# A fused encoder layer on one core: the FFN's matmul operands in two float16 parts with scales found on the chip, in place of two float32r parts

## The chip, the cores and the metric

One core of one Trainium2 chip runs the whole layer in one launch. The metric is device time in microseconds of that core, the median over timed runs. Engines are named as in the profile: PE (matmuls), PEld (weight loads of PE), DVE, ACT, POOL, and SP, which here only issues DMAs. "The DVE queue" and the like mean that an engine takes its instructions in one fixed order, so that an instruction that waits holds up all that stand behind it.

## What is computed

Sequence 1024, model width 1024, float32 in and out. The layer is an attention part (two kinds of heads, not touched here), a projection back to 1024, and then the part that this case is about:

```python
hn = rmsnorm(h, norm_ffn)
g = hn @ w_gate                      # 1024 x 2816
u = hn @ w_up                        # 1024 x 2816
g = conv3_depthwise(g, conv_w) + conv_b
h = h + (silu(g) * u) @ w_down       # 2816 x 1024
out = rmsnorm(h, norm_final)
```

The result has float32 accuracy, which one low-precision matmul doesn't give. So each operand is split into a high and a low part, and each block product is three matmuls: high times high, high weight times low operand, low weight times high operand.

## The kernel before

**Tiles.** Activations lie transposed: 128 features on the partitions, 1024 tokens along the row, in two halves of 512. Gate and up are taken together as a 2x2 block product by a scheme with seven products in place of eight (Strassen's, in a form with few sums). The same is done for the down projection. The 22 tiles of 128 hidden features ("units", class `Gated`) each take seven groups of matmuls, `p1` to `p7`, with 4 blocks of 128 in a group and three matmuls in a block (`group`, lines 956 to 961). That is 22 x 7 x 4 x 3 = 1848 matmuls with 512 columns. The down projection is seven products over 4 output tiles and 11 hidden tiles: 7 x 4 x 11 x 3 = 924 matmuls, the last 66 of them cut in two halves of 256 columns.

**Splits.** `split_w` (line 943) makes the two parts of a weight: ACT copies the float32 tile into a float32r tile (the high part, line 948), and DVE subtracts that from the float32 tile (the low part, line 949). `operand` (line 963) does this for the normalised activations, and `x_split` (line 1274) for the gated activations, which go through DRAM (`keep`, `x_load`) between the two projections. The sums that the seven products need (`ws`, `sum`, `t23`, `t4`) are DVE subtractions and additions ahead of the splits.

**Stages of the part in question**, with their place in the profile: the second half of the output projection with the residual and its sum of squares (lines 1017 to 1042; about 367 to 419 us); four head units taken phase by phase, while the activations of the second half of the tokens are still being made (to about 498 us); 18 units one after the other, each of which also prepares the weights of the next (class `Weights`, one step between two groups; to about 842 us); the down projection, where weights and gated activations are loaded some steps ahead (to 1051 us); and the final norm.

**What sets the order.** PE runs in program order (`manual_schedule` for PE). A scheduler orders the other engines' instructions and the DMAs of each queue when the program is built. Weights come through 9 buffers for the high and 9 for the low parts. PSUM banks have tags with two buffers each: `pj`, `o`, `s`, `pt`. In the down projection, product 1 adds onto the bank that still holds product 0, and product 0 itself is copied out for later use (`leave`).

Of the kernel before, what the change touches and what calls it, by code (L numbers as in the profile page):

```python
# [22 lines left out]
KT = D // 128  # L23
# [33 lines left out]
V_TOP, P_TOP, TINY = 2.0 ** 14, 2.0 ** 15, 1e-30  # L57

# [3 lines left out]
def hybrid_layer(tc, xT, w_in, w_out, w_gate, w_up, w_down, small, sink, rpb, consts, rope, out):  # L62
    nc = tc.nc
    with ExitStack() as ctx:
# [17 lines left out]
        def tmp(name, dt=F32, n=S):  # L82
            return tpool.tile([128, n], dt, name=name, tag="t", padded_shape=[128, S + 2])

# [858 lines left out]
        def split_w(src, n):  # L943

            pad = [128, 4, 128]
            hi = fpool.tile([128, n, 128], F32R, name="whi", tag="wh", bufs=9, padded_shape=pad)
            lo = fpool.tile([128, n, 128], F32R, name="wlo", tag="wl", bufs=9, padded_shape=pad)
            nc.scalar.activation(hi, src, AF.Copy)  # L948
            nc.vector.tensor_tensor(lo, src, f32(hi[:, :, :]), op=ALU.subtract)  # L949
            return [(hi[:, j, :], lo[:, j, :]) for j in range(n)]  # L950

        def load_raw(src, n):
            raw = fpool.tile([128, n, 128], F32, name="raw", tag="raw", bufs=3, padded_shape=[128, KT, 128])
            nc.sync.dma_start(raw, src)
            return raw

# [6 lines left out]
        def operand(src, tag):  # L963

            t = big("hg", tag, F32R)
            nc.scalar.activation(t[:, 0:HALF], src, AF.Copy)
            nc.vector.tensor_tensor(t[:, HALF:S], src, f32(t[:, 0:HALF]), op=ALU.subtract)
            return t[:, 0:HALF], t[:, HALF:S]
# [17 lines left out]
        def normed(h, wide, ds):  # L986
            for d in ds:
                nc.vector.scalar_tensor_tensor(at(d, h), at(d, h), col(C_NFFN + d), wide, op0=ALU.mult, op1=ALU.mult)

        def pure(f):  # L990
            raw = load_raw(w_gate[f], KT)
            W[f, "11"], W[f, "12"] = split_w(raw[:, 0:4], 4), split_w(raw[:, 4:8], 4)
# [8 lines left out]
        def head_weights(i, name):  # L1001
# [15 lines left out]
            W[f, name] = split_w(t, 4)  # L1017

        for h in range(2):
            for d in range(KT):  # L1020
# [9 lines left out]
                if h == 0 and d in (3, 4):  # L1030
                    pure((0, FT // 2)[d - 3])
                if h == 0 and d >= 5 or h == 1 and d == 0:
                    head_weights((d - 5) % KT, "s1")
# [10 lines left out]
        class Weights:  # L1044


            def __init__(self, f):
                self.f = f
                self.steps = [self.load, self.w11, self.w12, self.s1, self.s2, self.s4, self.s3, self.a22]

            def put(self, name, src):
                W[self.f, name] = split_w(src, 4)

            def load(self):
                self.g, self.u = load_raw(w_gate[self.f], KT), load_raw(w_up[self.f], KT)
# [33 lines left out]
        class Gated:  # L1089
# [32 lines left out]
            def conv(self):  # L1122
                f, gs = self.f, self.gs
                cw = lambda i: col(C_CW + 3 * f + i)
# [439 lines left out]
```

## Time and profile before

| | us |
|---|---|
| median of 3 runs (lowest, highest) | 1068.71 (1068.39, 1070.65) |
| the profiled execution, whole | 1067.82 |
| its span, first to last instruction | 1065.9 |
| PE busy | 1042.1 |
| DVE busy | 853.8 |
| ACT busy | 553.9 |
| POOL busy | 212.2 |

The mean granted clock of PE is 0.996. "Busy" is the time in which at least one instruction of the engine ran, by the profile's records. PE's records overlap, since matmuls are pipelined: a 512-column matmul is recorded with 0.39 us, while the next one starts 0.23 us after it. So matmuls are costed by the distance of their starts, and DVE's and ACT's instructions, which overlap a little too, by the length of an unbroken run of them divided by its count.

### The profile page before, as it was taken

To read this page: it belongs to the slowest core of one execution; us is meant where nothing else is said; L and a number is where in the kernel's file an instruction comes from. 1 tells how busy PE (TensorE), PEld (TensorE's weight loads), DVE (VectorE), ACT (ScalarE), POOL (GpSimd) and SP (SyncE) were. 2 spreads that over 40 slices of the span, in tenths; PEclk is the share of its full clock that TensorE was granted. 3 is DMA by queue.
4 is the path that set the end of the run, shared out by engine and by line. 5 is a ranking of instruction groups with operands and counts; after the bars stand their busy time and mean duration, and the time that the engine had idled before them with its cause. 6 is when DMAs were issued, how large, how long until landed. Compare 5 with 4: busy or idle time off the path is not lost.

```text
span 1065.9 us, 15180 instructions
## 1 busy us (share of the span) xinstructions
PE 1042.1 (98%) x4998; PEld 844.6 (79%) x4998; DVE 853.8 (80%) x1670; ACT 553.9 (52%) x1047; POOL 212.2 (20%) x312
## 2 busy tenths in 40 slices
PE   9989999999999999999999999999999999999997
PEld 7876777777777777787888888888888888888887
DVE  7789998767896789899988887887787858996764
ACT  8167787767686354454443433434334645544441
POOL 2234545767886200000000000000000000000002
PEclk9999999999999999999999999999999999999999
DMA  7236564877788273123433322223232789866644
GB/s 276 71 91 145 109 133 97 163 148 139 138 178 207 87 246 140 48 79 148 174 122 110 127 91 109 99 89 113 95 128 98 257 274 292 288 218 228 216 145 158
DMA packets 137358, 161.86 MB, mean 152 GB/s; under 512 B 76608, under 2 KB 87872, under 8 KB 137280
## 3 DMA queue, kind: packets, MB, share of 16 engines
q1 hardware_dynamic: 126624, 135.15, 45.0%
q10 hardware_dynamic: 10656, 25.76, 6.4%
q8 instruction: 39, 0.64, 0.2%
q14 instruction: 39, 0.32, 0.1%
HBM read 103.45 MB, written 28.57 MB: 124 GB/s over the span
## 4 chain that ended last, share of the span: by engine, by line
PE 69%; DVE 9%; DMA 2%; ACT 1%; issue 1%; POOL 1%; SPq 0%; DVEq 0%; ACTq 0%; POOLq 0%
PE dn L959 7%; PE dn L960 7%; PE dn L961 7%; PE z L961 5%; PE z L959 5%; PE z L960 5%; PE pj L157 4%; PE pj L159 4%; PE pj L158 4%; PE x L959 3%; PE x L960 3%; PE x L961 3%; PE y L961 3%; PE y L959 3%; PE y L960 3%; PE s L388 2%
## 5 line engine op out<-in xcount | busy, mean ns | idle before, releaser
L1385 POOL TENSOR_TENSOR h<-h,wide 128x256 f32<-128x256 f32 (+1 forms) x6 | 5.4, 919 | 624.7 <-ACT wide L1381 624.7
L948 ACT ACTIVATE whi<-ws 128x512 fp32r<-128x512 f32 (+1 forms) x100 | 60.2, 623 | 128.9 <-DVE ws L1065 82.5
L959 PE MATMUL dn<-xd,whi 128*128 128x512 f32 (+1 forms) x330 | 124.1, 376 | 0.0
L960 PE MATMUL dn<-xd,whi 128*128 128x512 f32 (+1 forms) x330 | 123.8, 375 | 0.0
L961 PE MATMUL dn<-xd,wlo 128*128 128x512 f32 (+1 forms) x330 | 123.7, 375 | 0.0
L157 PE MATMUL pj<-xgh,whi 128*128 128x512 f32 x248 | 107.2, 432 | 0.7 <-ACT whi L149 0.7
L961 PE MATMUL z<-hg,wlo 128*128 128x512 f32 x264 | 103.1, 390 | 0.6 <-DVE wlo L949 0.6
L959 PE MATMUL z<-hg,whi 128*128 128x512 f32 x264 | 103.0, 390 | 0.0
L960 PE MATMUL z<-hg,whi 128*128 128x512 f32 x264 | 102.8, 389 | 0.0
L159 PE MATMUL pj<-xgh,wlo 128*128 128x512 f32 x248 | 98.3, 396 | 1.4 <-POOL wlo L150 1.4
L158 PE MATMUL pj<-xgl,whi 128*128 128x512 f32 x248 | 97.9, 395 | 0.0
L422 ACT ACTIVATE p<-p,nm 128x385 f32<-128x385 f32 (+3 forms) x128 | 74.8, 585 | 39.7 <-DVE nm L418 34.8
L949 DVE TENSOR_TENSOR wlo<-ws,whi 128x512 fp32r<-128x512 f32 (+1 forms) x100 | 66.6, 680 | 18.1 <-ACT whi L948 18.0
L949 DVE TENSOR_TENSOR wlo<-raw,whi 128x512 fp32r<-128x512 f32 (+1 forms) x90 | 58.7, 673 | 22.7 <-ACT whi L948 20.8
L948 ACT ACTIVATE whi<-raw 128x512 fp32r<-128x512 f32 (+1 forms) x90 | 53.8, 615 | 38.6 <-DMA raw<-in_w_down_dram 10.4
L1277 ACT ACTIVATE xd<-xd 128x512 fp32r<-128x512 f32 x77 | 47.0, 625 | 46.4 <-DMA xd<-x 45.8
L960 PEld LDWEIGHTS dn<-xd,whi 128*128 128x128 f32 x330 | 62.1, 188 | 11.3 <-DVE xd L1278 0.2
L959 PEld LDWEIGHTS dn<-xd,whi 128*128 128x128 f32 x330 | 62.1, 188 | 11.2
L961 PEld LDWEIGHTS dn<-xd,wlo 128*128 128x128 f32 x330 | 62.1, 188 | 11.1
L1278 DVE TENSOR_TENSOR xd<-xd 128x512 fp32r<-128x512 f32 x77 | 51.8, 686 | 22.8 <-ACT xd L1277 22.6
L961 PE MATMUL y<-hg,wlo 128*128 128x512 f32 x176 | 68.7, 391 | 0.5 <-DVE wlo L949 0.5
L959 PE MATMUL x<-hg,whi 128*128 128x512 f32 x176 | 68.7, 390 | 0.0
(231 smaller groups left out, 2690.7 us busy)
## 6 DMA issues: line engine op xcount, KB each, us to landing
xd<-x SPq DMA_DIRECT2D x77, 256.0 KB, 4.7
raw<-in_w_down_dram SPq DMA_DIRECT2D x64, 256.0 KB, 3.9
raw<-in_w_gate_dram SPq DMA_DIRECT2D x22, 512.0 KB, 3.3
raw<-in_w_up_dram SPq DMA_DIRECT2D x22, 512.0 KB, 3.6
x<-c ACTq DMA_DIRECT2D x22, 512.0 KB, 2.7
raw<-in_w_in_dram SPq DMA_DIRECT2D x32, 256.0 KB, 3.2
raw<-in_w_down_dram SPq DMA_DIRECT2D x32, 192.0 KB, 4.0
x<-t ACTq DMA_DIRECT2D x11, 512.0 KB, 2.7
```

The costliest lines, as they stand in the source:

```text
L157: nc.tensor.matmul(ps, w[0], x[0][:, tsl(h)], start=first, stop=False)
L158: nc.tensor.matmul(ps, w[0], x[1][:, tsl(h)], start=False, stop=False)
L159: nc.tensor.matmul(ps, w[1], x[0][:, tsl(h)], start=False, stop=last)
L388: nc.tensor.matmul(ps[:, 0:n], qs, k[i][:, cs[0] * 128:cs[0] * 128 + n], start=i == 0, stop=i == 1)
L422: nc.scalar.activation(p[:, 0:e], p[:, 0:e], AF.Exp, bias=nm, scale=-1.0, accum_out=sm)
L948: nc.scalar.activation(hi, src, AF.Copy)
L949: nc.vector.tensor_tensor(lo, src, f32(hi[:, :, :]), op=ALU.subtract)
L959: nc.tensor.matmul(ps, w[0], x[0], start=first and i == 0, stop=False, skip_group_check=True)
L960: nc.tensor.matmul(ps, w[0], x[1], start=False, stop=False, skip_group_check=True)
L961: nc.tensor.matmul(ps, w[1], x[0], start=False, stop=last and i == len(ws) - 1, skip_group_check=True)
L1277: nc.scalar.activation(hi, f32(lo), AF.Copy)
L1278: nc.vector.tensor_tensor(lo, f32(lo), f32(hi), op=ALU.subtract)
```

## The change

Every operand of the FFN's and the down projection's matmuls becomes float16, still in two parts, and the three matmuls of a block stay. Since float16 has a small range, the operands are brought to fixed sizes by powers of two that are found on the chip:

- **Gate and up weights.** `weigh(f)` loads both 128x1024 weight tiles of a hidden tile a second time (`scan_rows`: a DMA on SP, and an ACT `Square` with a row sum); POOL adds the two sums. `settle_scale(f)` takes the largest over all partitions (`spread_max`: a transpose on PE, a reduction on DVE), forms the power -1/2 on POOL, and cuts the result to a power of two on DVE (`exponent`). It then forms `back` (its inverse) and `taps` (the convolution's weights times `back`) on DVE and POOL. `split_w` multiplies by the scale while it splits: ACT with a scale from a tile, DVE with `SCALAR_TENSOR_TENSOR` in place of `TENSOR_TENSOR`.
- **Norm gains.** `scale_gains` brings the FFN norm's gains to a fixed size, once; `operand` then splits the normalised activations without a scale, into a float16 pair.
- **Down weights.** One scale for all of `w_down`: 24 scans, two in each unit, and one `joint`.
- **Gated activations.** Each unit's result gets one more ACT `Square` with a row sum. Two scales come from these sums: one from all tiles but the last, ready for product 0, and one from all tiles. So product 1 can't add onto product 0 any more: it gets banks of its own, and four `add_first` more bring the two together. `add` takes its scale on the way (`SCALAR_TENSOR_TENSOR`).
- **Order in the source.** In the output projection, the first splits of gate weights come later (steps 6 and 7 in place of 3 and 4), since they wait for the scales.

```diff
-        def split_w(src, n):
+        def split_w(src, n, by):
...
-            hi = fpool.tile([128, n, 128], F32R, name="whi", tag="wh", bufs=9, padded_shape=pad)
-            lo = fpool.tile([128, n, 128], F32R, name="wlo", tag="wl", bufs=9, padded_shape=pad)
-            nc.scalar.activation(hi, src, AF.Copy)
-            nc.vector.tensor_tensor(lo, src, f32(hi[:, :, :]), op=ALU.subtract)
+            hi = fpool.tile([128, n, 128], F16, name="whi", tag="wh", bufs=9, padded_shape=pad)
+            lo = fpool.tile([128, n, 128], F16, name="wlo", tag="wl", bufs=9, padded_shape=pad)
+            nc.scalar.activation(hi, src, AF.Copy, scale=by)
+            nc.vector.scalar_tensor_tensor(lo, src, by, hi, op0=ALU.mult, op1=ALU.subtract)
...
+        def spread_max(v, tag):
+            ps = bank("wm", tag)
+            nc.tensor.transpose(ps[:, 0:128], v.to_broadcast([128, 128]), ident)
+            m = small("m")
+            nc.vector.tensor_reduce(m, ps[:, 0:128], axis=mybir.AxisListType.X, op=ALU.max)
+            return m
+        def scan_rows(dst, src, n=KT):
+            t = fpool.tile([128, n, 128], F32, name="scan", tag="scan", bufs=3, padded_shape=[128, KT, 128])
+            nc.sync.dma_start(t, src)
+            nc.scalar.activation(t, t, AF.Square, accum_out=dst)
+        def measure(v, tag):
+            s = spread_max(v, tag)
+            nc.gpsimd.tensor_scalar(s, s, FAINT, W_TOP ** -2, op0=ALU.max, op1=ALU.mult)
+            nc.gpsimd.tensor_tensor(s, s, minus_half[:, 0:1], op=ALU.pow)
+            exponent(s)
+            return s
...
+        def settle_scale(f, tag):
+            s = scale_of[f] = measure(row_of.pop(f), tag)
...
+            nc.vector.reciprocal(back, s)
+            nc.gpsimd.tensor_tensor(back, back, unit_back, op=ALU.mult)
+            nc.gpsimd.tensor_scalar(taps, par[:, C_CW + 3 * f:C_CW + 3 * f + 3], back, 1.0, op0=ALU.mult, op1=ALU.mult)
...
-                if h == 0 and d in (3, 4):
-                    pure((0, FT // 2)[d - 3])
-                if h == 0 and d >= 5 or h == 1 and d == 0:
-                    head_weights((d - 5) % KT, "s1")
+                if h == 0 and d < HEAD:
+                    for _ in weigh(FO[d]):
+                        pass
+                if h == 0 and d == 2:
+                    scale_gains()
+                if h == 0 and d >= HEAD:
+                    settle_scale(FO[d - HEAD], "pt")
+                if h == 0 and d >= 6:
+                    pure(FO[d - 6])
+                if (h, d) in S1_AT:
+                    head_weights(S1_AT.index((h, d)), "s1")
...
             def load(self):
+                settle_scale(self.f, self.tag)
                 self.g, self.u = load_raw(w_gate[self.f], KT), load_raw(w_up[self.f], KT)
...
-                nc.vector.tensor_tensor(u, u, self.cv, op=ALU.mult)
+                nc.vector.scalar_tensor_tensor(u, u, back_of[self.f], self.cv, op0=ALU.mult, op1=ALU.mult)
...
+                    nc.scalar.activation(junk, u, AF.Square, accum_out=x_rows[:, i:i + 1])
...
-            nc.scalar.activation(hi, f32(lo), AF.Copy)
-            nc.vector.tensor_tensor(lo, f32(lo), f32(hi), op=ALU.subtract)
+            nc.scalar.activation(hi, t[:, HALF:S], AF.Copy, scale=by)
+            nc.vector.scalar_tensor_tensor(lo, t[:, HALF:S], by, hi, op0=ALU.mult, op1=ALU.subtract)
...
+            if i == FT - HEAD - 3:
+                d_scale = joint(d_rows)
...
             if last_one:
+                x_scale.append(joint(x_rows[:, 0:FT - 1]))
+                x_back.append(inverse(x_scale[0], w_back))
...
-            nc.vector.tensor_tensor(x, ps[:, cols], x, op=ALU.add)
+            nc.vector.scalar_tensor_tensor(x, ps[:, cols], x_back[1], x, op0=ALU.mult, op1=ALU.add)
...
-            if p in (0, 2, 3) and c == 0:
-                banks[p, j] = bank("dn", tags(j, p == 2))
+            if p in (0, 1, 2, 3) and c == 0:
+                banks[p, j] = bank("dn", tags(j, p in (1, 2)))
...
+            if i == 4:
+                x_scale.append(joint(x_rows))
+                x_back.append(inverse(x_scale[1], w_back))
```

Three places in the built order matter for what follows.

SP's queue at the output projection. `raw<-in_w_out_dram` are the projection's own weights, which PE needs one after the other, and `raw<-in_w_gate_dram` and `raw<-in_w_up_dram` are FFN weights. Before:

```order
L911 DMA raw<-in_w_out_dram 128x512 x4
L954 DMA raw<-in_w_gate_dram 128x1024
L911 DMA raw<-in_w_out_dram 128x512
L954 DMA raw<-in_w_gate_dram 128x1024
L911 DMA raw<-in_w_out_dram 128x512
L954 DMA raw<-in_w_up_dram 128x1024 x4
```

And now, where `scan` are the loads of `scan_rows`:

```order
L917 DMA raw<-in_w_out_dram 128x512
L980 DMA scan<-in_w_gate_dram 128x1024
L980 DMA scan<-in_w_up_dram 128x1024
L917 DMA raw<-in_w_out_dram 128x512
L980 DMA scan<-in_w_gate_dram 128x1024
L980 DMA scan<-in_w_up_dram 128x1024
L917 DMA raw<-in_w_out_dram 128x512
L980 DMA scan<-in_w_gate_dram 128x1024
L917 DMA raw<-in_w_out_dram 128x512
L980 DMA scan<-in_w_up_dram 128x1024
L980 DMA scan<-in_w_gate_dram 128x1024
L917 DMA raw<-in_w_out_dram 128x512
```

The last six loads of the projection's weights, which stood in front but for two loads, now each have one or two scan loads of twice their size ahead of them; there are 3 buffers for scans, each given back when ACT has squared its tile.

DVE's queue at the turn from one unit to the next, in the stage with one unit after the other. Before:

```order
L1133 TENSOR_TENSOR c<-z,c 128x512
L1128 SCALAR_TENSOR_TENSOR cv<-gs,par,cv 128x1023
L949 TENSOR_TENSOR wlo<-raw,whi 128x512 x2
L1109 TENSOR_TENSOR c<-y,c 128x512
L1138 TENSOR_TENSOR c<-z,c 128x512
L1139 TENSOR_TENSOR c<-c,cv 128x1024
```

And now:

```order
L1211 TENSOR_TENSOR c<-z,c 128x512
L955 SCALAR_TENSOR_TENSOR wlo<-ws,m,whi 128x512
L955 SCALAR_TENSOR_TENSOR wlo<-raw,m,whi 128x512
L974 TENSOR_REDUCE m<-wm 128x1
L967 TENSOR_SCALAR m<-m 128x1
L1006 RECIPROCAL back<-m 128x1
L1187 TENSOR_TENSOR c<-y,c 128x512
L955 SCALAR_TENSOR_TENSOR wlo<-raw,m,whi 128x512 x2
L1216 TENSOR_TENSOR c<-z,c 128x512
L1217 SCALAR_TENSOR_TENSOR c<-c,back,cv 128x1024
```

The reduction L974 waits for PE's transpose, and L967 right behind it waits for the two POOL instructions that work on the reduction's result; all that follows on DVE waits with them, among it L1187, which takes `y` out of PSUM. In some units two to four other instructions stand between L974 and L967.

PE's queue in the last unit, where the first scale of the gated activations is formed (`wm` is the transpose):

```order
L1027 MATMUL x<-hg,whi 128x512
L1028 LDWEIGHTS whi
L1028 MATMUL x<-hg,whi 128x512
L1029 LDWEIGHTS wlo
L1029 MATMUL x<-hg,wlo 128x512
L972 MATMUL wm<-cst,v 128x128
L1027 LDWEIGHTS whi
L1027 MATMUL z<-hg,whi 128x512
```

The transpose stands between two groups, so the groups behind it wait for the last `Square` but one. Weight loads of float16 matmuls are instructions of their own here; those of float32r matmuls came with the matmul. There are 26 such transposes in all, 5 of them in the output projection.

113 lines of the change are left out of this document (91 added, 22 removed).

## The prediction

> **What bounds the kernel now.** First the page: busy shares, slices, chain.
>
> ```profile
> PE 1042.1 (98%) x4998; PEld 844.6 (79%) x4998; DVE 853.8 (80%) x1670; ACT 553.9 (52%) x1047; POOL 212.2 (20%) x312
> DVE  7789998767896789899988887887787858996764
> PEclk9999999999999999999999999999999999999999
> PE 69%; DVE 9%; DMA 2%; ACT 1%; issue 1%; POOL 1%; SPq 0%; DVEq 0%; ACTq 0%; POOLq 0%
> ```
>
> PE runs nearly without a gap at full clock and holds 69% of the chain of waits, so the distance between matmul starts sets the time. DVE is second, and near full in some slices. So I asked for windows by stage (columns: length, then busy us and instructions of PE, PEld, DVE, ACT, POOL, then PE clock, DMA share, GB/s): the projection (360 to 420), inside the head units (440 to 480), the head units with the turn to the single units (419 to 504), the single units (504 to 842), the down projection (842 to 1051).
>
> ```profile
> 360.00:420.00 60.00, 56.90 (x259) 45.76 (x258) 53.38 (x89) 26.24 (x44) 4.35 (x3) 1.00 0.46 158
> 440.00:460.00 20.00, 20.00 (x90) 16.57 (x89) 20.00 (x34) 9.48 (x17) 0.00 (x0) 1.00 0.00 1
> 460.00:480.00 20.00, 20.00 (x89) 16.29 (x88) 20.00 (x30) 10.86 (x15) 0.00 (x0) 1.00 0.31 106
> 419.00:504.00 85.00, 83.82 (x371) 68.15 (x369) 78.81 (x121) 40.09 (x63) 1.38 (x1) 1.00 0.28 99
> 504.00:842.00 338.00, 337.33 (x1485) 278.24 (x1484) 275.85 (x390) 137.49 (x209) 0.00 (x0) 1.00 0.33 118
> 842.00:1051.00 209.00, 209.00 (x977) 175.03 (x976) 155.46 (x259) 100.34 (x176) 2.55 (x2) 1.00 0.71 237
> ```
>
> In the single units and the down projection PE alone is the bound. In the head units DVE is as full as PE (20.00 of 20): a faster PE finds nothing ready there.
>
> **A. Matmuls: what float16 saves.** Timeline of PE, first and last row of a run each: eight float32r matmuls with 512 columns, eight with 256, and float16 ones with 256 in runs of two and of four.
>
> ```profile
> 551.71 0.39 PE L961 MATMUL y<-hg,wlo 128*128 128x512 f32 x1
> ...
> 553.30 0.39 PE L959 MATMUL z<-hg,whi 128*128 128x512 f32 x1
> ...
> 1040.24 0.28 PE L961 MATMUL dn<-xd,wlo 128*128 128x256 f32 x1
> ...
> 1041.08 0.28 PE L959 MATMUL dn<-xd,whi 128*128 128x256 f32 x1
> ...
> 100.24 0.39 PE L477 MATMUL o<-turned,v 128*128 128x256 f16 x2
> ...
> 101.17 0.61 PE L477 MATMUL o<-turned,v 128*128 128x256 f16 x4
> ```
>
> Float32r: (553.30 - 551.71) / 7 = 0.227 us with 512 columns, (1041.08 - 1040.24) / 7 = 0.120 with 256. So 256 columns more cost 0.107, and 0.013 is fixed. Float16: two more in a run add 0.61 - 0.39, so 0.110 each with 256 columns. No row has float16 with 512. Bounds: 0.110 + 0.107 = 0.217, or twice 0.110, 0.220, if nothing of it is fixed; below, the rounding of the rows allows 0.215. I take 0.2165, near the first, since the fixed part was seen in the other type. (The Trainium skill, "TensorE: Matmul & The Clock Gate", section "Back-to-back issue gap", gives columns / 2.4 + 2.5 ns warm, 215.8 ns here: by it the saving would be 32 us in all. The same section names 131 ns as sustained for 512; the row of float16 with 256 columns at 0.110 speaks against that.)
>
> Changed are 1848 + 858 matmuls with 512 columns and 132 with 256: 2706 x 0.0105 + 132 x 0.010 = 28.4 + 1.3 = **29.7 us less** (20 to 34 by the bounds).
>
> **B. Transposes on PE.** 26 are added.
>
> ```profile
> 303.42 0.49 PE L450 MATMUL pt<-cst,p 128*128 128x128 f32 x3
> L450 PE MATMUL pt<-cst,p 128*128 128x128 f32 x136 | 23.0, 275 | 3.6 <-DVE turned L454 1.3 <-POOL p L426 1.3 <-POOL p L417 1.1
> ```
>
> Three take 0.49, one 0.275: (0.49 - 0.275) / 2 = 0.108 each. With 0.01 for the change of type: 26 x 0.12 = **3.1 us more** (up to 6, if the queue waits 0.1 at each).
>
> **C. DVE's and ACT's prices.** Runs of DVE in its timeline, then groups:
>
> ```profile
> 409.19 2.49 DVE L967 TENSOR_TENSOR hg<-h,hg 128x512 fp32r<-128x512 f32 x4
> 432.35 2.72 DVE L988 SCALAR_TENSOR_TENSOR h<-h,par,sw 128x512 f32<-128x512 f32 x4 [0.30 <-PE sw L219]
> L198 DVE TENSOR_REDUCE v<-st 128x4 f32<-128x512 f32 x8 | 5.3, 684 | 1.1 <-PE st L196 1.0
> L200 POOL TENSOR_TENSOR v<-v,minus_half 128x4 f32<-128x4 f32 x8 | 9.8, 1228 | 75.2 <-DVE v L199 75.1
> L306 POOL TENSOR_TENSOR gains<-par,up 128x1 f32<-128x1 f32 x8 | 1.9, 245 | 0.2
> L186 ACT ACTIVATE sq<-xt 128x1024 f32<-128x1024 f32 x8 | 8.2, 1047 | 0.0
> L422 ACT ACTIVATION_READ_ACCUMULATOR p<-p,nm 128x1 f32 x128 | 24.0, 187 | 0.0
> L644 ACT ACTIVATE xgh<-xt,par 128x512 fp32r<-128x512 f32 x4 | 2.7, 706 | 0.0
> L1277 ACT ACTIVATE xd<-xd 128x512 fp32r<-128x512 f32 x77 | 47.0, 625 | 46.4 <-DMA xd<-x 45.8
> ```
>
> Four `TENSOR_TENSOR` take 2.49, one 0.68, so (2.49 - 0.68) / 3 = 0.60 each in a run; `SCALAR_TENSOR_TENSOR` (2.72 - 0.74) / 3 = 0.66. Each low part costs 0.06 more. A scale costs DVE 0.34: a reduction of 128 columns (a quarter of L198's, say 0.20) and two narrow ones at 0.07. Between reduction and exponent DVE waits for POOL: 0.25 (L306) + 1.23 (L200) + hand-overs, some 1.9 us, less where other work stands between.
>
> ACT pays 0.08 more for each high part (706 against 625) and 1.05 + 0.19 for each scan and each `Square` of a gated tile. Per single unit that is 7 x 0.08 + 5 x 1.24 = 6.8 us, beside 137.49 / 17.75 = 7.7 now: 14.5 of 18.3 us. It is hidden behind PE; what it could delay is in the rivals.
>
> **D. Single units: taken as nothing.** 338 / 19.04 (84 x 0.2267) = 17.75 units. DVE has 275.85 now. A unit adds 8 x 0.06 + 0.34 = 0.8, and a wait of 1.9 in about half of them, 1.0 on average (1.9 at most): 275.9 + 17.75 x 1.8 = 308 us, of 338 - 1485 x 0.0105 + 2 = 324 for PE. PE stays the bound by 16 us; the 9 weight buffers of each kind keep weights about a unit ahead. If that cover is gone: up to 8.
>
> **E. Head units: 5.5 us of the saving don't arrive.** Between 419 and 504, A counts 371 x 0.0105 = 3.9 us, and PE would need 81.1. DVE has 78.81 of 85 now; the 22 low parts of weights formed there add 1.3 (DVE's groups of this window), and two scales with their waits some 3: 83.1 us if all its 6.2 us of idle time can be used, 89.3 if none. So the stretch takes 83.1 to 89.3, against the 81.1 that A assumes: 2.0 to 8.2 lost. I take 5.5, a little above the middle, because the rows from 440 to 480 have no idle time left to use. What is late is the evacuation of `y` and `z`, and the low parts of `s3` and `s2`, for which PE then waits.
>
> ```profile
> L949 DVE TENSOR_TENSOR wlo<-ws,whi 128x512 fp32r<-128x512 f32 x13 | 8.7, 682 | 0.6 <-ACT whi L948 0.6
> L949 DVE TENSOR_TENSOR wlo<-raw,whi 128x512 fp32r<-128x512 f32 x9 | 6.1, 687 | 2.2 <-PE st L196 1.3 <-ACT whi L948 0.9
> ```
>
> **F. Output projection: 2.5 us.** DVE has 53.38 of 60 and gets five scales with little between reduction and exponent: 5 x 1.8 = 9, so 62.4. On SP, the last six loads of the projection's weights now stand behind scans. PE waits for these weights today:
>
> ```profile
> 377.20 0.50 PE L159 MATMUL pj<-mgh,wo 128*128 128x512 f32 x1 [0.48 <-DVE wo L914]
> 392.58 0.50 PE L159 MATMUL pj<-mgh,wo 128*128 128x512 f32 x1 [0.83 <-DVE wo L914]
> 370.86 6.69 SPq L911 DMA_DIRECT2D raw<-in_w_out_dram  x4
> 380.00:400.00 20.00, 18.84 (x83) 14.95 (x82) 15.94 (x27) 9.47 (x17) 0.00 (x0) 1.00 0.84 285
> ```
>
> From 370.9, 8 scans with 4.2 MB and six loads with 1.6 MB are to pass: 20 us at 285 GB/s, while PE wants the last of them after 7 x 2.8 = 20 (12 matmuls at 0.23 for each). Bounds 0 and 6; I take 2.5, from DVE's overflow.
>
> **G. Down projection: 1.5 us.** At most 77 gated splits, 84 weight splits and 26 additions get dearer by 0.06 each, 11 us; 155.46 + 11 + 4 x 0.6 for `add_first` + 2 x 2.2 for the scales = 173 on DVE, of 199: PE stays the bound. But the transpose in the last unit waits for a unit's product, its `Square` and a reduction (twice 0.60, 1.24 and 0.20, behind queued work), with two groups, 5.2 us, as cover, and DVE stands still twice for POOL. Bounds 0 and 4.
>
> **Sum:** -29.7 + 3.1 + 0 + 5.5 + 2.5 + 1.5 = -17.1. The profiled execution took 1067.8 as a whole (span 1065.9), so 1050.7; the median of the runs lies 0.9 above it. **1051 us.**
>
> **Rivals.**
>
> 1. *The head's cover holds.* E, F and G vanish: PE's queue absorbs DVE's lateness, as it does now at 440 to 480 without a wait. -29.7 + 3.1 gives 1041. Against it: DVE's sum for the head units is over PE's. Chance 0.20.
> 2. *The projection stalls behind the scans.* ACT, SP and the 3 scan buffers form a ring, and the projection's weights wait in it. F at 6 and E at 8, with G at 4: 1059. Chance 0.12.
> 3. *POOL's narrow instructions hold up DVE.* For: the group below takes 1.06 us for a shape that costs 0.74 elsewhere, in a stage where POOL is busy. Five POOL instructions per unit, about 2.3 us, would be added to DVE: 275.85 / 17.75 = 15.5, + 0.8 + 2.3 = 18.6 a unit against 18.3; 17.75 x 0.3 = 5 more, 1056. (The Trainium skill, "SBUF — State Buffer", section "SBUF: two separate sides", has a lock behind it: a DVE instruction with two SBUF inputs and a POOL instruction that reads SBUF exclude each other. The group agrees; that it holds for such narrow ones no run here shows.) Chance 0.08.
>
> ```profile
> L284 DVE SCALAR_TENSOR_TENSOR kb<-t,cst,ka 128x512 fp32r<-128x512 f32 x16 | 16.8, 1058 | 1.0 <-ACT ka L283 0.7
> ```
>
> 4. *Slower: DVE becomes the bound in the single units.* Its idle time now, (338 - 275.85) / 17.75 = 3.5 us a unit, isn't spare but part of a ring with ACT (high part before low part, gate before convolution), with its place at the turn from unit to unit. If half of it stays: 15.5 + 0.8 + 1.9 + 1.75 = 20.0 against 19.04 now, 17.75 x 0.96 = +17; with the head at +4 against now and the down projection at -8: 1081. It ends slower than before from about 19.3 us a unit. Against it: most weights have a unit's time. Chance 0.10.
> 5. *Float16 with 512 columns is no faster than 0.227,* and the saving is one of 256 columns alone. The rest stays: 1068 + 3 + 3 = 1074. Against it: the fixed part in the rows. Chance 0.05.
>
> **The numbers.** Forecast 0.45; rivals 0.20, 0.12, 0.08, 0.10, 0.05. Its own range is 1045 to 1056. The range takes in rivals 1 to 3: 1037 to 1063. Less than 0.2% is about what a measurement here can't tell from no change: faster 0.84, same 0.02, slower 0.14 (4, 5, less a little).
>
> **What would show it.** Step A: starts 0.216 to 0.217 apart in the single units. B: the transposes' group at 26 records, without waits. D: a unit in 18.2 to 18.4 us, with PE idle near 0 from 540 on. E: DVE full from the first `y` to the turn, PE waiting for low parts or `y` and `z`. F: PE waiting for `wo`. G: a wait of at most 2 us at the first down product. The prediction is wrong if starts lie at 0.227, if units take over 18.6 us, or if the head units end over 8 us later than PE's own work there would let them.

## The result and the profile after

The changed kernel takes 1078.99 us (median of 4 runs, 1076.12 to 1081.54), against 1068.55 for the kernel before (4 runs, 1067.46 to 1070.65). The ratio is 1.0091, with a 95% interval of 1.0073 to 1.0110: it is slower by 0.9%. The forecast was 1051 (1037 to 1063). The profiled execution has a span of 1074.3 us and is the fastest of the four, so what is read from it below falls some 3 us short of the median.

First the page of the changed kernel, with the lines for the same things as before:

```profile
PE 1024.9 (95%) x5024; PEld 601.4 (56%) x5024; DVE 885.2 (82%) x1757; ACT 669.8 (62%) x1227; POOL 264.0 (25%) x432
DVE  6789998767896768799998888888888879998674
PEclk9999999999999999899999999999999999999998
PE 55%; DVE 12%; DMA 9%; ACT 5%; issue 2%; POOL 1%; SPq 0%; ACTq 0%; DVEq 0%; POOLq 0%
```

PE's share of the chain of waits fell from 69% to 55% and DMA's rose from 2% to 9%. In two of the 40 slices of the granted clock, the 17th (430 to 457 us) and the last, the digit is 8; before, it was 9 in all.

The same windows as before, of the changed kernel (the times are the same, but its stages begin 5 to 20 us later, so a window doesn't hold quite the same work; length, then busy us and instructions of PE, PEld, DVE, ACT, POOL, then PE clock, DMA share, GB/s):

```profile
360.00:420.00 60.00, 54.81 (x246) 42.63 (x245) 45.69 (x88) 35.61 (x62) 14.66 (x27) 1.00 0.78 283
440.00:460.00 20.00, 17.97 (x86) 8.46 (x87) 16.72 (x28) 16.56 (x32) 1.57 (x2) 1.00 0.60 204
460.00:480.00 20.00, 20.00 (x95) 9.04 (x94) 19.35 (x32) 12.80 (x24) 0.19 (x1) 1.00 0.63 203
419.00:504.00 85.00, 74.50 (x322) 33.95 (x321) 74.19 (x116) 60.57 (x105) 2.14 (x5) 0.94 0.62 206
504.00:842.00 338.00, 331.53 (x1543) 151.39 (x1541) 295.96 (x454) 201.69 (x312) 38.35 (x86) 1.00 0.49 168
842.00:1051.00 209.00, 202.88 (x926) 91.45 (x927) 173.12 (x277) 121.27 (x190) 2.97 (x7) 0.98 0.72 234
```

Look at the fourth row. Before, PE and DVE were both nearly full there (83.82 and 78.81 of 85). Now both have room, and what grew is the transfers: 206 GB/s against 99. Neither engine is full in the head units any more; both wait for something.

To see where time was lost, the program is cut at three places that both kernels have: the first `x` (the head units begin), the fifth unit's first `x` (the single units begin), and the first `dn`. First PE's timeline of the kernel before, then of the changed kernel:

```profile
419.38 0.39 PE L959 MATMUL x<-hg,whi 128*128 128x512 f32 x1
498.29 0.39 PE L959 MATMUL x<-hg,whi 128*128 128x512 f32 x1
843.24 0.39 PE L959 MATMUL dn<-xd,whi 128*128 128x512 f32 x1
```

```profile
424.32 0.39 PE L1027 MATMUL x<-hg,whi 128*128 128x512 f16 x1
517.88 0.38 PE L1027 MATMUL x<-hg,whi 128*128 128x512 f16 x1
852.36 0.38 PE L1027 MATMUL dn<-xd,whi 128*128 128x512 f16 x1
```

The forecast by stage is the stage before with the prediction's own terms: A split by matmuls (3.9 head, 15.6 single, 10.2 down), B by transposes at 0.12 (5, 20, 1), and E, F and G where they belong.

| stage (us) | before | forecast | measured | over |
|---|---|---|---|---|
| up to the first `x` | 419.4 | 422.5 | 424.3 | 1.8 |
| head units | 78.9 | 80.5 | 93.6 | 13.1 |
| single units | 344.9 | 331.7 | 334.5 | 2.8 |
| from the first `dn` to the end | 222.7 | 214.1 | 221.9 | 7.8 |
| span | 1065.9 | 1048.8 | 1074.3 | 25.5 |

Two stages hold 20.9 of the 25.5 us. Both have their own chain of waits. The other two rows, 1.8 and 2.8, are smaller than what such a cut can tell, as is shown below.

**The head units.** PE's longest wait there is for an addition on DVE. Timelines of PE, ACT, DVE and SP of the changed kernel (the bracket gives the idle time ahead and what ended it):

```profile
431.48 0.58 PE L1027 MATMUL x<-hg,whi 128*128 128x512 f16 x1 [4.40 <-DVE h L1046]
431.87 0.63 PE L1028 MATMUL x<-hg,whi 128*128 128x512 f16 x1
432.29 0.63 PE L1029 MATMUL x<-hg,wlo 128*128 128x512 f16 x1
```

```profile
419.13 1.06 ACT L981 ACTIVATE scan<-scan 128x1024 f32<-128x1024 f32 x1 [1.93 <-DMA scan<-in_w_up_dram]
420.19 0.61 ACT L1034 ACTIVATE hg<-h 128x512 f16<-128x512 f32 x1
```

```profile
420.83 0.69 DVE L1035 TENSOR_TENSOR hg<-h,hg 128x512 f16<-128x512 f32 x1 [2.01 <-ACT hg L1034]
```

```profile
411.52 0.38 SPq L980 DMA_DIRECT2D scan<-in_w_up_dram  x1
412.45 3.01 SPq L980 DMA_DIRECT2D scan<-in_w_down_dram  x2
...
423.05 0.33 SPq L980 DMA_DIRECT2D scan<-in_w_down_dram  x1
424.67 0.33 SPq L960 DMA_DIRECT2D raw<-in_w_gate_dram  x1
429.67 0.33 SPq L980 DMA_DIRECT2D scan<-in_w_down_dram  x1
...
433.38 6.30 SPq L960 DMA_DIRECT2D raw<-in_w_gate_dram  x3
```

And SP's queue in the waits view, from 419 to 518 us (waited for: us, times, longest):

```profile
SPq L980 <- ACT scan L981: 51.1, 19, 6.4
```

Read them upward from SP. Scans are issued between the head's raw weights, scans of `w_down` among them, whose scale is used 400 us later. SP stands still for 51.1 us in all until ACT's `Square` has freed a scan buffer, and the raw weights behind it stand too. On ACT, a `Square` waits 1.93 us for its load; the high part of an operand stands behind it; DVE waits 2.01 for that high part, then works without a gap until it reaches `h` (L1046), for which PE waits 4.40. So the 2.01 are a part of the 4.40; how much of the rest is the scans' isn't read from these rows. From 431.87 on the matmuls start 0.42 to 0.43 apart (432.29 is the next) instead of 0.216, twelve of them: behind the wait PE runs at half its clock. The end of the stage has one more wait, 3.26 us at 517.72, of a scale's transpose for a bank of PSUM; it is taken up with the experiments.

**The down projection.** SP's queue in the waits view, from 860 to 1045 us (waited for: us, times, longest); before first, then changed:

```profile
SPq L1247 <- DVE sum L1265: 30.3, 22, 2.8
SPq L1247 <- DVE ws L1265: 22.8, 5, 7.4
SPq L1271 <- PE dn L961: 8.2, 10, 5.4
```

```profile
SPq L1362 <- DVE sum L1380: 40.1, 27, 3.3
SPq L1362 <- DVE ws L1380: 23.9, 6, 7.3
SPq L1386 <- PE dn L1029: 2.5, 7, 0.6
```

L1247 and L1362 are the loads of raw weights: they wait for DVE to have formed sums from one of the three raw buffers. In SP's one order the loads of gated tiles (L1271, L1386) stand behind them. This ring ran in the kernel before too, and PE had no gap there; now it waits more for DVE, and hardly for PE. PE's waits for `dn` from 843 to 1050 us come to 4.9 us, and over half of it is this one:

```profile
PE dn L1027 <- ACT whi L954: 2.7, 2, 2.4
```

With 13 matmuls at half clock, 2.7 us, that is 7.6 of the 9.3 us lost in the stage (7.8 over the forecast, and 1.5 that the forecast has in G).

### The profile page after: what moved, and what is told of

The parts are those of the page before. It is cut to its first block, busy times and chain, and to the rows that moved or that the text cites. A ratio compares the mean times of both kernels' runs of the same rounds, so it can differ in the third digit from the quotient of the medians.

```text
span 1074.3 us, 15755 instructions
## 1 busy us (share of the span) xinstructions
PE 1024.9 (95%) x5024; PEld 601.4 (56%) x5024; DVE 885.2 (82%) x1757; ACT 669.8 (62%) x1227; POOL 264.0 (25%) x432
## 4 chain that ended last, share of the span: by engine, by line
PE 55%; DVE 12%; DMA 9%; ACT 5%; issue 2%; POOL 1%; SPq 0%; ACTq 0%; DVEq 0%; POOLq 0%
PE dn L1029 5%; PE dn L1027 5%; PE dn L1028 5%; PE z L1029 4%; PE z L1027 4%; PE z L1028 4%; PE pj L163 4%; PE pj L165 3%; PE pj L164 3%; DMA scan<-in_w_up_dram 3%; DVE wlo L955 2%; DMA xd<-x 2%; PE y L1029 2%; PE y L1028 2%; PE y L1027 2%
## 5 line engine op out<-in xcount | busy, mean ns | idle before, releaser
L1029 PEld LDWEIGHTS <-wlo 128*128 128x128 f16 x946 | 93.3, 99 | 114.8 <-issue 5.5
L1028 PEld LDWEIGHTS <-whi 128*128 128x128 f16 x946 | 93.3, 99 | 114.5 <-issue 12.9
L1027 PEld LDWEIGHTS <-whi 128*128 128x128 f16 x946 | 93.6, 99 | 113.4 <-ACT whi L954 6.6
L1027 PE MATMUL dn<-xd,whi 128*128 128x512 f16 (+1 forms) x330 | 121.5, 368 | 3.5 <-ACT whi L954 2.7
L1028 PE MATMUL dn<-xd,whi 128*128 128x512 f16 (+1 forms) x330 | 121.8, 369 | 0.9 <-DVE xd L1394 0.9
L1029 PE MATMUL dn<-xd,wlo 128*128 128x512 f16 (+1 forms) x330 | 121.9, 369 | 0.5 <-DVE wlo L955 0.5
L1027 PE MATMUL z<-hg,whi 128*128 128x512 f16 x264 | 101.5, 385 | 2.5 <-ACT whi L954 1.9
L1029 PE MATMUL z<-hg,wlo 128*128 128x512 f16 x264 | 101.5, 384 | 1.8 <-DVE wlo L955 1.8
L1028 PE MATMUL z<-hg,whi 128*128 128x512 f16 x264 | 101.4, 384 | 0.0
L954 ACT ACTIVATE whi<-ws,m 128x512 f16<-128x512 f32 (+1 forms) x100 | 68.6, 708 | 37.2 <-DVE ws L1143 21.8
L981 ACT ACTIVATE scan<-scan 128x1024 f32<-128x1024 f32 (+1 forms) x68 | 69.6, 1024 | 24.9 <-DMA scan<-in_w_up_dram 13.6
L955 DVE SCALAR_TENSOR_TENSOR wlo<-ws,m,whi 128x512 f16<-128x512 f32 (+1 forms) x100 | 72.8, 743 | 11.8 <-ACT whi L954 11.5
L1027 PE MATMUL x<-hg,whi 128*128 128x512 f16 x176 | 68.0, 386 | 5.3 <-DVE h L1046 4.4
L1028 PE MATMUL x<-hg,whi 128*128 128x512 f16 x176 | 67.9, 386 | 0.0
```

What stands on the lines that cost most here:

```text
L954: nc.scalar.activation(hi, src, AF.Copy, scale=by)
L955: nc.vector.scalar_tensor_tensor(lo, src, by, hi, op0=ALU.mult, op1=ALU.subtract)
L981: nc.scalar.activation(t, t, AF.Square, accum_out=dst)
L1027: nc.tensor.matmul(ps, w[0], x[0], start=first and i == 0, stop=False, skip_group_check=True)
L1028: nc.tensor.matmul(ps, w[0], x[1], start=False, stop=False, skip_group_check=True)
L1029: nc.tensor.matmul(ps, w[1], x[0], start=False, stop=last and i == len(ws) - 1, skip_group_check=True)
```

## The experiments

Times below are medians, with the ratio to the kernel before and its 95% interval. The stages are cut as above; each row's cuts come from its own timeline of PE, of one execution. How far such a cut can be read is shown by "changed" and "changed, six buffers": up to 837 us PE, DVE and SP have the same instructions in the same order in both, and yet the time to the first `x` differs by 3.2 us and the single units by 3.0, while the head is 93.6 in both. So a difference of some 3 us in one row of one stage tells nothing by itself.

| kernel | to first `x` | head | single | rest | span | median, ratio |
|---|---|---|---|---|---|---|
| before | 419.4 | 78.9 | 344.9 | 222.7 | 1065.9 | 1068.55 |
| changed | 424.3 | 93.6 | 334.5 | 221.9 | 1074.3 | 1078.99, 1.0091 (1.0073 to 1.0110) |
| constant scales | 417.7 | 78.5 | 328.7 | 224.0 | 1049.0 | 1050.62, 0.9831 (0.9795 to 0.9866) |
| no scans | 422.4 | 82.9 | 334.9 | 222.7 | 1062.9 | 1064.79, 0.9973 (0.9956 to 0.9990) |
| Squares alone | 424.6 | 81.2 | 339.7 | 225.7 | 1071.1 | 1070.92, 1.0014 (0.9997 to 1.0031) |
| loads alone | 426.1 | 91.1 | 334.5 | 224.8 | 1076.5 | 1075.78, 1.0064 (1.0047 to 1.0082) |
| constant, six buffers | 419.0 | 77.2 | 328.9 | 211.9 | 1037.1 | 1038.88, 0.9723 (0.9684 to 0.9762) |
| constant, POOL's queue | 416.6 | 78.5 | 328.7 | 228.3 | 1052.2 | 1055.93, 0.9882 (0.9823 to 0.9942) |
| late scans | 423.1 | 82.9 | 337.4 | 222.6 | 1066.0 | 1067.47, 0.9994 (0.9980 to 1.0007) |
| changed, six buffers | 427.5 | 93.6 | 331.5 | 213.5 | 1066.2 | 1064.31, 0.9960 (0.9947 to 0.9973) |
| late scans, moved transposes | 423.1 | 79.8 | 334.3 | 226.0 | 1063.3 | 1066.46, 1.0002 (0.9986 to 1.0017) |
| late, spread scans | 423.6 | 84.3 | 335.1 | 220.7 | 1063.6 | 1067.86, 1.0002 (0.9989 to 1.0014) |
| all four | 423.8 | 79.3 | 333.3 | 217.7 | 1054.1 | 1057.12, 0.9912 (0.9887 to 0.9937) |

### Constant scales: float16 by itself

```diff
-            settle_scale(self.f, self.tag)
+        scale_of, back_of = {f: w_by for f in range(FT)}, {f: unit for f in range(FT)}
...
-                    nc.scalar.activation(junk, u, AF.Square, accum_out=x_rows[:, i:i + 1])
```

> The changed kernel with every scale a constant: no scans of weights, no Square of the gated tiles, no transposes, no chain on VectorE and GpSimd; float16 and its three products stay. Theory (the lost time comes from the scales' way of being found, first of all from the scans on SyncE's queue): step A stands alone, starts 0.216 us apart, span 1038 to 1044, head units as long as PE's own work (about 76 us from the first x to the first single unit). Rival (float16 itself, dearer low parts on VectorE, or a ring of buffers that a faster PE only uncovers, hold the kernel): 1050 or more, with the stalls in the head or from 1000 us on still there.

Measured 1050.6: 28.4 us below the changed kernel, but 12 above what float16 alone should give (1068.6 - 29.7), and the span, 1049.0, misses the expected 1038 to 1044. The single units are as float16 alone should make them (328.7; 344.9 - 15.6 = 329.3), the head is 3.5 longer (78.5; 78.9 - 3.9); the down projection, with nothing but constants, is no shorter than before (224.0 against 222.7). So two causes, and the theory is half right: the scales cost, and something in the down projection, which the experiments on its buffers below show to be a ring, takes float16's saving there.

### The scans, and their two halves

```diff
-            nc.sync.dma_start(t, src)
-            nc.scalar.activation(t, t, AF.Square, accum_out=dst)
+            nc.gpsimd.memset(dst, 1.0)                                  # no scans
...
+            nc.scalar.activation(scan_out[:, 0:n], scan_in[:, 0:n], AF.Square, accum_out=dst)     # Squares alone
...
+            nc.sync.dma_start(t, src); nc.gpsimd.memset(dst, 1.0)       # loads alone
```

> The changed kernel without the 68 scans alone (loads and Squares of the weights left out, the row sums set to 1); transposes, reductions, powers, exponents and the Square of the gated tiles stay. If the scans are what costs: 1042 to 1050, within some 5 us of the kernel with constant scales. If the chain reduction - power - exponent is what costs: 1060 or more.

> The changed kernel with the scans' Squares on ScalarE over a tile that stays, and no scan loads. If SyncE's queue and the DMA are the scans' price (my theory): 1045 to 1053, near the kernel without scans. If ScalarE's queue is (high parts and Squares in one order): over 1062.

> The changed kernel with the scans' 68 loads and without their Squares (row sums set to 1). Theory (queue and DMA): 1065 to 1080, near the changed kernel. If ScalarE's Squares are the price: under 1055.

Without scans 1064.8: the scans cost 14.2 us, and finding the scales from them costs as much again against constant scales (14.2). I had expected almost all of it in the scans (1042 to 1050), so that expectation failed. The kernel with the Squares alone missed too: 1071, expected 1045 to 1053 if the queue of SP were the whole price. The kernel with the loads alone, 1075.8, came out as expected. In the head the table separates the halves: 82.9 without scans, 91.1 with the loads, 81.2 with the Squares. There the loads are the price, also without a `Square` in ACT's queue: SP then waits 43.9 us, from 419 to 518, for scans to land before it issues the next (against 51.1 for ACT above). Over the whole kernel the loads cost 11.0 and the Squares 6.1, so the Squares aren't free; together they cost 14.2, less than the sum. The longest wait in that profile's single units is one for ACT, 5.29 us at 519.54, with 12 matmuls at half clock behind it. The changed kernel has no wait over 0.81 there, so that part needn't hold for it.

The other 14.2, the chains', lies ahead of the down projection: by the table 4.7 up to the first `x`, 4.4 in the head, 6.2 in the single units, and -1.3 in the rest. Waits of PE in the kernel without scans (us in total, times, longest), and its timeline:

```profile
PE wm L972 <- DVE v L1253: 4.0, 2, 3.1
PE wm L972 <- DVE c L1214: 3.3, 1, 3.3
PE sw L225 <- POOL v L206: 2.9, 2, 2.3
```

```profile
505.14 0.32 PE L972 MATMUL wm<-cst,rg 128*128 128x128 f32 x1 [3.26 <-DVE c L1214]
```

`wm` is a scale's transpose. It stands in PE's order and waits 3.3 us at the turn to the single units for a bank of PSUM that a head unit still holds, and 3.1 us in the last unit for the gated tiles' maxima (L1253); behind both, PE's timeline shows matmuls 0.427 apart, 7 and 6 of them. Either wait with the half-clock matmuls of its stage (7 and 13 between the cuts, at 0.21 each) gives 4.7 and 5.8 us, near the 4.4 and 6.2. The third row isn't the chains' alone: with constant scales PE waits 1.7 us there.

### Late scans

```diff
+            with behind(*["head"] * ("head" in mark)):
                 nc.sync.dma_start(t, src)
...
+        mark["head"] = mark["raw"]
         w_next = Weights(FO[HEAD], "pj")
```

> The changed kernel with every scan that the program issues after the head units' last weight load also held behind that load on SyncE's queue; nothing else differs. If the scans that ran ahead into the head units cost the time there: from the first x to the first single unit 82 to 87 us instead of 93.6, the whole 1066 to 1072. If the eight scans for the head's own scales, or VectorE's chains, cost it: 91 to 95 and 1076 to 1081.

Head units 82.9, the whole 1067.5. What moved is shown by the order on SP, from the first difference on, of the changed kernel and of the one with late scans (an order, not times; `raw` are the weights that the head units need):

```text
231 L980 DMA scan_6120<-in_w_gate_dram 128x1024
232 L960 DMA raw_5404<-in_w_gate_dram 128x1024
233 L960 DMA raw_5476<-in_w_gate_dram 128x1024
234 L980 DMA scan_6142<-in_w_up_dram 128x1024
235 L980 DMA scan_6164<-in_w_down_dram 128x1024
236 L980 DMA scan_6197<-in_w_down_dram 128x1024
237 L980 DMA scan_6282<-in_w_gate_dram 128x1024
238 L980 DMA scan_6304<-in_w_up_dram 128x1024
239 L980 DMA scan_6345<-in_w_down_dram 128x768
240 L960 DMA raw_5596<-in_w_gate_dram 128x512
```

```text
231 L960 DMA raw_5404<-in_w_gate_dram 128x1024
232 L960 DMA raw_5476<-in_w_gate_dram 128x1024
233 L960 DMA raw_5596<-in_w_gate_dram 128x512
234 L960 DMA raw_5617<-in_w_gate_dram 128x512
```

The same bytes, the same instructions, another place: 25 scans, written in the program behind the head units, stood on SP ahead of the head's last weight load. Holding them back takes 10.7 us off the head, all that leaving the scans out takes off it (82.9 in both), and 11.5 off the median. It also takes their transfers out of the head, so place and shared transfers have to be told apart by the traces: a raw gate load of 256 KB took 4.2 us to land beside the scans and 3.0 without them (medians from 419 to 504 us), while the last five raw loads of the head go out from 496.07 on, against 484.63 with late scans. 11.4 us later is nearly the whole price, so it is the place in the main; that the shared transfers have no part in it isn't shown. (The scheduler also ordered some of DVE's and ACT's instructions otherwise in this kernel.)

### The ring of the down projection

```diff
-            raw = fpool.tile([128, 2, n, 128], F32, name="raw", tag="raw", bufs=3, ...)
+            raw = fpool.tile([128, 2, n, 128], F32, name="raw", tag="raw", bufs=6, ...)                    # constant scales
+            raw = fpool.tile([128, 2, n, 128], F32, name="raw", tag=("raw", "scan")[loaded[0] % 2], bufs=3, ...)   # changed
...
-            tc.keep_in_program_order(nc.sync.dma_start(t[:, HALF:S], X[PRODUCTS[p][1], k]))
+            nc.gpsimd.dma_start(t[:, HALF:S], X[PRODUCTS[p][1], k])                                        # POOL's queue
```

> Constant scales, and six buffers instead of three for raw weights (room that the scans no longer take). In the kernel with constant scales the down projection took 214.7 us of span against 213.7 before, so float16 saved nothing there. Theory: the ring of three raw buffers (a load waits on SyncE's queue until VectorE has formed a sum from the buffer, and the loads of gated tiles stand behind it) paces it: with six, 203 to 207, the whole 1039 to 1044. Rival (DMA's rate or VectorE's work): still 213 to 215, the whole 1048 to 1052.

> Constant scales, three raw buffers, and the 77 loads of gated tiles issued from GpSimd's queue instead of SyncE's. If the gated tiles come late because they stand behind loads that wait for a buffer: down projection 203 to 208, the whole 1040 to 1045. If the three raw buffers alone pace it: 213 to 215 and 1048 to 1052.

> The changed kernel with the down projection's raw weights in six buffers (its three and the scans' three, which are free by then); nothing else. If the ring of raw buffers took the saving there also beside the scans: down projection 203 to 206 us instead of 213.0, the whole 1067 to 1072. If with scales from the chip something else holds it (the dearer splits on VectorE, the two joint scales): 210 to 213, the whole 1076 or more.

Six buffers take 12.1 us off the rest with constant scales and 8.4 with scales from the chip. (By the medians it is 11.7 and 14.7 off the whole; of the 14.7 the two profiled executions, 1076.1 and 1068.0, show 8.1.) With six buffers the rest takes 211.9 and 213.5, about what the forecast had for it, 214.1. Another queue for the gated tiles takes nothing off (228.3 against 224.0; the median, 1055.9, lies above both expected ranges), so it isn't their place behind blocked loads alone. With six buffers, SP's queue in the changed kernel waits as follows:

```profile
SPq L1386 <- PE dn L1029: 38.5, 9, 11.1
```

Now the loads of gated tiles wait 38.5 us for PE to free their buffers, where they waited 2.5: loads run ahead. PE has no wait for `dn` left, with either kind of scales, so PE is the bound again. (The kernel with constant scales has six buffers in all stages, and its 77.2 in the head against 78.5 may come from that.)

### Moved transposes, spread scans, and all together

```diff
-            more()
+            if i:
+                more()
             u.p1()
             more()
             u.p5()
+            if not i:
+                more()
...
                 u.p7()
+                x_scale.append(joint(x_rows[:, 0:FT - 1]))
...
-                if h == 0 and d < HEAD:
+                if h == 0 and d % 2 == 0:
```

> The kernel with the late scans, and two transposes of scales moved in TensorE's order: that of the second single unit behind the first one's y and z, that of the down projection's first scale behind one more product. With late scans TensorE waited 3.2 us and 2.6 us there, and ran at half clock for 8 matmuls each time. Theory (a wait for a buffer of PSUM and for VectorE, which later places hide): single units and down together 5 to 9 us shorter, 1059 to 1063. Rival (what was waited for comes late for the next matmuls instead): 1065 to 1069.

> The kernel with the late scans, and the eight scans of the head units in every second step of the output projection instead of the first four, with the scales of the third and fourth unit two to four products later. Theory (scans and the projection's weights compete there for the transfers): output projection 65 to 66 us instead of 68.1, the whole 1063 to 1066. Rival (the head units then wait for their scales): the projection shorter, the head longer by as much, 1066 to 1070.

> Late scans, six raw buffers in the down projection, moved transposes and spread scans together. If the causes are separate: 1067.5 - 10 (ring) - 7 (transposes) - 2 (spread) = 1048, range 1044 to 1053. If one hides another: 1055 or more.

The moved transposes shortened the head and the single units by 6.2 us together, but the rest grew by 3.4 and the median fell by only 1.0: the number is the rival's. (The waits named in that expectation are counted from start to start; as idle time they are 2.86 and 2.23.) Another wait took part of it back; PE's timeline of that kernel:

```profile
852.32 0.48 PE L972 MATMUL wm<-cst,v 128*128 128x128 f32 x1 [4.38 <-DVE v L1256]
```

This is the second scale of the gated tiles, behind the first four groups of the down projection. Behind it 13 matmuls run at half clock. Spreading the scans, expected to take 2 to 3 us off the projection, changed nothing that can be told (to the first `x` 423.6 against 423.1). All together give 1057.12, which beats the kernel before by 0.9% with scales still found on the chip. It isn't the 1048 of a plain sum: the wait at the second scale is still there (4.0 us), and the rest is 4.9 shorter than with late scans alone, where six buffers took off 8.4 above.

## Why the prediction was wrong

**A, right.** Starts lie 0.2158 apart (group of `x` at 552.74, of `y` at 555.33: 2.59 / 12), forecast 0.2165. With the ring widened and constants for scales the kernel takes 0.9723 of the time before, some 29 us less: nearly the whole term arrives. Rival 5 is out with it.

```profile
552.74 0.38 PE L1027 MATMUL x<-hg,whi 128*128 128x512 f16 x1
...
555.33 0.38 PE L1027 MATMUL y<-hg,whi 128*128 128x512 f16 x1
...
570.98 0.38 PE L1027 MATMUL x<-hg,whi 128*128 128x512 f16 x1
...
589.22 0.38 PE L1027 MATMUL x<-hg,whi 128*128 128x512 f16 x1
```

**B, a failed step: right in its size, wrong in what it left out.** A transpose takes 0.11 of PE (552.63 to 552.74 in the timeline). But it is an instruction in PE's order with two conditions of its own, a free bank and a row of maxima. Costed by its duration, with 0.1 us of waiting as a bound, it came out at 3.1 to 6; one single wait was 3.3 without scans, and 3.26 in the changed kernel too, inside the head's 13.1. The chains as a whole, of which B is the part on PE, cost 14.2.

**C and D, right.** Groups of the changed kernel:

```profile
L955 DVE SCALAR_TENSOR_TENSOR wlo<-ws,m,whi 128x512 f16<-128x512 f32 x96 | 70.7, 748 | 11.7 <-ACT whi L954 11.5
L974 DVE TENSOR_REDUCE m<-wm 128x1 f32<-128x128 f32 x26 | 7.4, 284 | 0.8 <-PE wm L972 0.8
L967 DVE TENSOR_SCALAR m<-m 128x1 int32<-128x1 int32 x26 | 4.0, 152 | 17.1 <-POOL m L987 17.1
```

A low part is dearer by 0.063 (748 against 685 for the 96 of the same kind before); DVE's wait for POOL is 17.1 / 26 = 0.7, against 1.0 assumed. A unit takes 18.24 us (570.98 to 589.22), forecast 18.2 to 18.4. DVE has 295.96 of 338, below the 308 forecast (in the stage itself, 517.88 to 852.36, it is 291.35 of 334.48). Rivals 3 and 4 didn't come: they need units of 18.6 and 20.0 us. Rival 4's time, 1081, lies nearest to the measured one, but by luck. The 2.8 us over are no more than one wait at the turn to the down projection with 7 matmuls at half clock behind it, 4.1 us:

```profile
842.75 0.32 PE L972 MATMUL wm<-cst,v 128*128 128x128 f32 x1 [2.60 <-DVE v L1255]
```

**E, the first failed step: right for what it counted; it left a queue out.** Windows of the kernel with constant scales:

```profile
419.00:504.00 85.00, 79.33 (x365) 35.11 (x363) 81.71 (x122) 42.64 (x64) 1.01 (x1) 1.00 0.29 99
440.00:460.00 20.00, 20.00 (x94) 9.10 (x93) 20.00 (x34) 8.07 (x15) 0.00 (x0) 1.00 0.00 1
460.00:480.00 20.00, 17.66 (x82) 7.67 (x80) 20.00 (x30) 11.34 (x14) 0.00 (x0) 1.00 0.36 114
```

DVE is full and PE waits, and 78.5 us is 3.5 above 78.9 - 3.9. That is E's mechanism, within E's bounds. In the changed kernel it didn't get that far, because SP's order had 25 scans in the head: 93.6 us, where PE's own work would take 75.0, far beyond the 8 us that the prediction named as a sign of being wrong. The failed step is the sentence of E that names only DVE's 22 low parts and two scales: in C a scan was costed as 1.24 us on ACT ("It is hidden behind PE"), and in F its load, for eight scans only. What the load of a scan does to the loads behind it on SP, in the head, was put at nothing; it measured 10.7 us. Rival 2 (1059) comes near, with SP and the scan buffers in a ring with ACT; but it has that ring in the projection and 8 us for the head, and the loads alone cost 8.2 there without any `Square` in the ring.

**F.** 1.8 us over, inside its bound of 6, and too small to be told from one profile. Its sign came: PE waits for `wo` five times, 4.1 us in all, where it waited twice, 1.3, before. Without scans it waits once, 0.5, but the stage is still 3.0 longer than before; PE then waits 2.29 at `sw` (L225) in this stage, where it waits 1.00 in the changed kernel. So the scans' part is seen, and its worth in the stage isn't settled.

**G, the second failed step.** "173 on DVE, of 199: PE stays the bound." DVE has 173.12 in the window, which in the changed kernel begins 10 us ahead of the stage; shifted to the stage (851.1 to 1060.1) it has 171.03. The sum was right to some 2 us and the conclusion wrong by 7.8 us: it compared busy times, and the stage was held by a ring of three buffers, in which no engine is full. It was visible before: SP's queue waited 53 us for DVE's sums there, the rows shown above, and no step of the prediction uses them. The wait expected at the first down product was at the scale's transpose instead, the 2.60 us above.

**The clock, not in the prediction.** In the changed kernel 39 matmuls of the FFN start 0.40 to 0.44 us apart, on average 0.426. At 0.210 each above their normal distance that is 8.2 us, a third of the 25.5. The waits of 4.40 and 2.60 us shown above are followed by such stretches, the one of 3.26 at 517.72 isn't: where a stretch comes, it is a price on top of the wait. The last section has more on it.

## What to carry to other kernels

An extra read of data isn't priced by the engine that does something with it. Ask the queue that issues the load what will stand behind it, and how far ahead a scheduler will move it when nothing holds it back; here holding 25 loads back was worth 10.7 us of the head units, with the same loads and instructions. When the bound engine gets faster, price the rings next to it (buffers, the load that waits for one, the engine that frees it), by the waits of the issuing queue: a stage can be held with every engine's busy sum below its length.

## What the hardware showed unasked

In these traces PE's clock halves after idle time, and the length of a wait alone doesn't decide it; where it lay does too. In one kernel a wait was put by hand into each single unit:

```diff
+            nc.tensor.transpose(ps[:, 0:128], w_by.to_broadcast([128, 128]), ident)
+            nc.scalar.activation(t, ps[:, 0:128], AF.Copy)
+            for _ in range(i % 9):
+                nc.gpsimd.tensor_tensor(t, t, held, op=ALU.mult)
+            nc.tensor.transpose(ps[:, 128:256], t[:, 0:1].to_broadcast([128, 128]), ident)
```

> Constant scales, and in each single unit a wait of TensorE put in by hand: a transpose, a copy on ScalarE, 0 to 8 multiplications on GpSimd, and a transpose that needs them. Waits of 1 to 6 us. Theory (TensorE's clock falls after it has been idle, whatever the reason): matmuls start 0.43 us apart for some 3 us behind each wait above about 2.3 us, 0.216 behind the short ones. Rival (the half speed seen behind stalls in the changed kernel comes from transfers or from SBUF): 0.216 behind all.

It took 1139.11 us in its one run. Two of its waits, from PE's timeline:

```profile
568.41 0.32 PE L1339 MATMUL wm<-cst,probe 128*128 128x128 f32 x1 [2.68 <-POOL probe L1338]
...
589.52 0.32 PE L1339 MATMUL wm<-cst,probe 128*128 128x128 f32 x1 [2.56 <-POOL probe L1338]
```

Behind the longer one matmuls start 0.216 apart at once; behind the shorter one 8 of them start 0.427 apart. The times at which the full clock comes back agree, within 0.3 us, with one grid of 3.414 us through the whole execution (13 of them, from 481 to 1106 us). Windows on that grid:

```profile
563.20:566.61 3.41, 2.53 (x13) 1.02 (x10) 3.37 (x6) 2.08 (x4) 0.43 (x1) 1.00 0.17 42
566.61:570.03 3.42, 1.62 (x8) 0.84 (x9) 3.38 (x5) 0.72 (x1) 1.59 (x3) 1.00 0.30 116
570.03:573.44 3.41, 3.41 (x17) 1.56 (x16) 2.32 (x4) 0.72 (x1) 0.00 (x0) 1.00 0.00 0
587.09:590.50 3.41, 0.97 (x5) 0.55 (x6) 0.80 (x2) 0.25 (x1) 1.81 (x4) 1.00 0.00 0
590.50:593.92 3.42, 3.42 (x10) 1.31 (x9) 0.00 (x0) 0.00 (x0) 0.00 (x0) 0.54 0.00 0
```

The longer wait is split over two windows, idle for 0.9 and 1.8 us of 3.41, and nothing happens. The shorter one lies in one window, idle for 2.44, and the next window runs at half clock (0.54 granted), though PE is busy in all of it. Over this execution, at full clock, a window idle for 2.4 us or more was always followed by the slow clock, one idle for 1.8 or less never; between (2.0 to 2.2) it went either way. So my expectation, every wait over 2.3 us, was wrong in its rule (2.02 at 770.88 was followed by half clock, 3.08 at 818.00 wasn't), and right in that no transfer is needed: the DMA share is 0.00 in the last two windows. (The Trainium skill, "TensorE: Matmul & The Clock Gate", section "What's actually happening", gives a free-running window of 3413 ns, with which the grid agrees. It has the clock fall after at least one idle window, and the section "HAM oscillation — how this bites in real kernels" warns of gaps over some 3.4 us. Here windows that were two thirds idle were enough, and waits of 2.0 to 2.6 us.) It isn't float16's: in the kernel without scans, six float32r matmuls of the output projection start 0.426 to 0.427 apart from 408.1 to 410.2 us, behind a wait of 2.29. So a wait of 2 to 3 us here cost up to about 1.7 us (8 x 0.21) more than itself, or nothing more, by the place where it fell. That this widens the spread of the kernels with such waits is likely, but wasn't tried.
